# A two-block transformer layer pair on one core: the first projection begun chunk by chunk in all eight PSUM banks

## The chip, the core and the metric

One core of one Trainium2 chip runs the whole kernel. The metric is the device time of one execution in microseconds (us). The engines are TensorE (PE; its weight loads are listed as PEld), VectorE (DVE), ScalarE (ACT), GpSimd (POOL) and SyncE (SP, which here only issues DMAs).

## The reference, cut to what matters

Two layers run one after the other on 256 tokens of width 2048, all float32. The change lies in the front of the first layer:

```python
mod = silu(c) @ w_ada + b_ada                      # c: 2048, w_ada: 2048 x 6144
shift, scale, gate = split(mod, 3)
h = rms_norm(x, g_norm) * (1 + scale) + shift      # x: 256 x 2048
proj = h @ w_in                                    # w_in: 2048 x 9296
qa, ka, va, za, q_idx, k_idx, w_idx, qb, kb, vb, zb = split(proj)
# ka, qa, kb, qb, k_idx are rms-normalised per head; q_idx, k_idx, w_idx score the keys, the
# 64 best stay; two attentions, gates silu(za), silu(zb), @ w_out, residual
```

The second layer (mixer with forgetting attention, pooling, a convolutional feed-forward block) is not touched.

## The kernel before, in words

**Number format.** A float32 product is made of three faster ones. `wload` (L193) loads a weight tile of 128 x 1024 by one DMA on SP's queue into one of 8 raw buffers `wr` (L186), ACT copies it into a rounded high part `wh` (L198), and DVE subtracts for a low part `wl` (L199); there are 4 buffers of each. Activations are split in the same way into pairs `ap`. `mm3` (L222) then issues three matmuls: high x high (L226), high x low (L227), low x high (L228).

**The modulation.** `ada(col)` (L345) computes 128 columns of `mod`: two loads of 512 KB of `w_ada` (`wr`, L348), and for each a multiply-and-sum on DVE (L349, tile `junk`) against `cB`, the vector silu(c) spread over the partitions by PE (L321) and DVE (L322). `make_h(k)` (L358) builds chunk k (128 of the 2048 features) of h: two small sums (L353), the normed x times the gain (`xh`, L362), high part and full value on ACT (L364, L365), low part on DVE (L366). Chunk k needs the columns k and 16 + k, so four loads, 2.1 MB.

**The norm.** x arrives in four loads (L465). ACT squares 16 chunks (L248), PE sums them by products with a matrix of ones (L269), ACT and DVE make 1/sqrt (L273 to L280).

**The first projection.** The 16 chunks are cut into groups of 3, 4, 4 and 5 (`KS`, L37). Within a group the output is made block by block, 512 columns each: two blocks of q_idx (`fq_block`, L417), then ten of ka, qa, va, kb, qb (`tm_block`, L396), each over all chunks of the group. PSUM has eight banks: four `mm` (L177), two `sc` (L180), two `tp` (L183). The sums of ka stay in `sc` and `tp` through all groups; every other block takes two of the `mm` banks and is added to a copy in SBUF at the end of each group (`acc_add`, L373: a copy on ACT, L376, in the first group, an addition on DVE, L379, afterwards). `merge` (L439) spreads the `ada` and `make_h` steps of the next group evenly between the blocks of this one, so that a group starts with all its chunks of h.

**After it.** In the last group `ki_block` (L429, k_idx and w_idx) comes first, then q_idx and the ten blocks, with the index scores (L504), the eight rounds that find the 64 best keys (`topk_round`, L528) and the head norms (L539) between the blocks; then the gates za in eight pieces (`z_chunk`, L609), vb, attention, and the rest.

The order on each engine is chosen at build time by a scheduler that simulates the program; `keep` (L160) pins an instruction to its place in the source. Each engine executes its instructions in that order, and a wait holds up all behind it.

Of the kernel before, what the change touches and what calls it, by code (L numbers as in the profile page):

```python
# [11 lines left out]
F32 = mybir.dt.float32  # L12
# [135 lines left out]
def tile_hybrid_layers(ctx: ExitStack, tc: tile.TileContext, i: dict, out: bass.AP, dbg=None):  # L148
# [12 lines left out]


# [30 lines left out]
    def wload(src, n=1024):  # L193

        r_ = wraw(src, n)
        h = wp.tile([P, 1024], F32R, name="wh", tag="wh", bufs=HI)
        lo = wp.tile([P, 1024], F32R, name="wl", tag="wl", bufs=LO)
        nc.scalar.copy(h[:, :n], r_[:, :n])  # L198
        nc.vector.tensor_tensor(lo[:, :n], r_[:, :n], h[:, :n].bitcast(F32), op=ALU.subtract)  # L199
        return h, lo  # L200

# [109 lines left out]
    for _ in range(8):  # L311
        nc.tensor.matmul(ps[:, :P], ones, ones, start=True, stop=True)
# [4 lines left out]
    for j in range(4):  # L317
        ps = ps_mm()
        for q in range(4):
            k = 4 * j + q  # L320
            nc.tensor.matmul(ps[:, q * P:q * P + P], sc[:, 1, k:k + 1].to_broadcast([P, P]), ident, start=True, stop=True)  # L321
        nc.vector.tensor_scalar(cB[:, j // 2, (j % 2) * 512:(j % 2) * 512 + 512], ps, 0.5, None, op0=ALU.mult)  # L322
# [16 lines left out]
    nc.vector.tensor_scalar(qg[:, 0:1], v("qna"), P ** -0.5, None, op0=ALU.mult)  # L339
    nc.vector.tensor_scalar(qg[:, 1:2], v("qnb"), P ** -0.5, None, op0=ALU.mult)  # L340
# [4 lines left out]
    def ada(col):  # L345

        for hf in range(2):
            w = wraw(i["wada"][col, hf])  # L348
            nc.vector.tensor_tensor_reduce(junk[hf], w, cB[:, hf, :], 1.0, 0.0, op0=ALU.mult, op1=ALU.add,  # L349
                                           accum_out=mpart[:, col, hf:hf + 1])  # L350
# [7 lines left out]
    def make_h(k):  # L358
        mod_sum(k, 1)
        mod_sum(16 + k, 1)  # L360
        x = tmp("xh")[:, :T]
        nc.vector.scalar_tensor_tensor(x, r[:, k, NM:], v("gnorm", k), RINV[0], op0=ALU.mult, op1=ALU.mult)  # L362
# [4 lines left out]
        hA[k] = (h, lo)  # L367

# [12 lines left out]
    early = {}  # L381

    def k_tiles(src, k0, n):

        k = k0
        while k < k0 + n:
            m = min(2, k0 + n - k)
            yield [(k + j, j * 512) for j in range(m)], early.pop((id(src), k), None) or w_at(src, k, m)
            k += m
# [26 lines left out]

    def fq_block(g, b, src, k0, n):  # L417
# [21 lines left out]
    def merge(a, b):  # L439

        done = 0
        for n, f in enumerate(a):
            want = (n + 1) * len(b) // len(a)
            while done < want:
                b[done]()
                done += 1
            f()

    def group_steps(g):
        k0, n = KGROUPS[g]  # L450
        st = [lambda b=b: fq_block(g, b, w1q[b], k0, n) for b in range(2)]
        tm = [lambda b=b: tm_block(g, TMB[b // 2][0], b % 2, i["w1t"][b], k0, n) for b in range(10)]
        return st + tm

    def ada_steps(g):
        def last(k):
            ada(16 + k)
            make_h(k)

        k0, n = KGROUPS[g]  # L460
        return [f for k in range(k0, k0 + n) for f in (lambda k=k: ada(k), lambda k=k: last(k))]

    w1q = [i["w1q"][b] for b in range(2)]
    for j in range(4):
        nc.sync.dma_start(r[:, 4 * j:4 * j + 4, NM:], i["xT"][:, 4 * j:4 * j + 4, :])  # L465
    warm_ln()
    RINV[0] = rsqrt_of((square(r[:, k, NM:], T) for k in range(KC)), KC, T)
    st = ada_steps(0)
    for f in st[:-1]:
        f()  # L470
    early[id(w1q[0]), 0] = w_at(w1q[0], 0, 2)
    st[-1]()
# [6 lines left out]
    steps = group_steps(NG - 1)  # L479
# [57 lines left out]
    heads = {}  # L537

    def head_norm(key, gain):  # L539

        nss = sp.tile([P, 16], F32, name="nss", bufs=2)
        nrs = sp.tile([P, 16], F32, name="nrs", bufs=2)
        for blk in range(2):
            for f in range(2):
                a = acc[key, blk, f].rearrange("p a b -> p (a b)")
                for h in range(4):
                    sqt = tmp("sq")
                    at = blk * 8 + f * 4 + h
                    nc.scalar.activation(sqt[:, :P], a[:, h * P:h * P + P], AF.Square, accum_out=nss[:, at:at + 1])
        nc.vector.tensor_scalar(nss, nss, 1.0 / P, EPS, op0=ALU.mult, op1=ALU.add)  # L550
        nc.gpsimd.tensor_tensor(nrs, nss, neghalf, op=ALU.pow)
        for blk in range(2):
            av = [acc[key, blk, f].rearrange("p a b -> p (a b)").rearrange("p (h d) -> p h d", h=4) for f in range(2)]
            for f in range(2):
                at = blk * 8 + f * 4
                nc.vector.tensor_tensor(av[f], av[f], nrs[:, at:at + 4, None].to_broadcast([P, 4, P]), op=ALU.mult)
            for pr in range(2):
                t = ps_t()
                for h in range(2):
                    for f in range(2):  # L560
                        nc.tensor.transpose(t[:, h * T + f * 128:h * T + f * 128 + 128], av[f][:, 2 * pr + h, :], ident)  # L561
                d = bank("hT")
                nc.scalar.activation(d.rearrange("p a b -> p (a b)"), t, AF.Copy, scale=gain)
                heads[key, 4 * blk + 2 * pr] = d[:, 0, :]
                heads[key, 4 * blk + 2 * pr + 1] = d[:, 1, :]

# [6 lines left out]
    for s_ in steps[:4]:  # L573
        s_()
    ki_transpose()
    blocks = steps[4:]
    ih = 0
    for b in range(8):
# [9 lines left out]
        if 4 <= b < 8:  # L588
            topk_round()
            topk_round()  # L590
        if b == 0:
            head_norm("ka", v("kna"))
        if b == 2:
            head_norm("qa", qg[:, 0:1])
        if b == 6:
            head_norm("kb", v("knb"))
    topk_end()
# [53 lines left out]
    for zi in range(8):  # L651
        z_chunk(zi)
    for b in range(2):
# [55 lines left out]
    nc.vector.tensor_scalar(bqs, v("bq", 0, 8), P ** -0.5, None, op0=ALU.mult)  # L709
# [158 lines left out]
    nc.vector.tensor_scalar(hb, v("bga", 0, 32), 0.5, None, op0=ALU.mult)  # L868
# [210 lines left out]
```

## Time and profile before

| | |
|---|---|
| median of 3 runs | 1965.72 us (1965.16 to 1966.75) |
| the profiled execution, its own time | 1966.43 us |
| its span in the trace | 1964.7 us |
| PE busy | 1930.4 us (98%) |
| DVE busy | 1316.2 us (67%) |
| ACT busy | 975.7 us (50%) |
| mean granted TensorE clock | 0.992 of full speed |
| chain that ended last | PE 96%, DVE 2%, DMA 1% |

The execution's own time is 1.7 us above its span, and 0.7 us above the median of the runs. Matmuls are pipelined: the row of one gives its time in the pipe, and what it costs in a stream is the step from one start to the next. A float32 product that is not split shows as two rows. Times within the trace count from the start of the span.

### The profile page before, as it was taken

To read this page: it belongs to the slowest core of one execution; us is meant where nothing else is said; L and a number is where in the kernel's file an instruction comes from. 1 tells how busy PE (TensorE), PEld (TensorE's weight loads), DVE (VectorE), ACT (ScalarE), POOL (GpSimd) and SP (SyncE) were. 2 spreads that over 40 slices of the span, in tenths; PEclk is the share of its full clock that TensorE was granted. 3 is DMA by queue.
4 is the path that set the end of the run, shared out by engine and by line. 5 is a ranking of instruction groups with operands and counts; after the bars stand their busy time and mean duration, and the time that the engine had idled before them with its cause. 6 is when DMAs were issued, how large, how long until landed. Compare 5 with 4: busy or idle time off the path is not lost.

```text
span 1964.7 us, 34265 instructions
## 1 busy us (share of the span) xinstructions
PE 1930.4 (98%) x13760; PEld 1810.9 (92%) x13760; DVE 1316.2 (67%) x2063; ACT 975.7 (50%) x1537; POOL 19.4 (1%) x27
## 2 busy tenths in 40 slices
PE   6999999999999999999999999999999999999997
PEld 5888878889999999999999998999998899999886
DVE  7899788786675445755546648877764467777544
ACT  4644376466464445544444446644444454545542
POOL 0000011000000000000000000000000000000000
PEclk7999999999999999999999999999999999999999
DMA  9999685774555444556666664556666655555662
GB/s 340 353 348 348 215 265 180 286 279 148 173 165 161 140 146 130 176 183 183 183 182 183 182 182 140 185 181 183 182 184 192 193 185 181 181 182 183 206 190 87
DMA packets 126367, 391.35 MB, mean 199 GB/s; under 512 B 14400, under 2 KB 16576, under 8 KB 126208
## 3 DMA queue, kind: packets, MB, share of 16 engines
q1 hardware_dynamic: 125552, 387.83, 61.6%
q8 instruction: 108, 1.77, 0.4%
q10 hardware_dynamic: 576, 1.05, 0.1%
q14 instruction: 51, 0.42, 0.1%
q0 software_dynamic: 80, 0.28, 0.0%
HBM read 387.01 MB, written 2.10 MB: 198 GB/s over the span
## 4 chain that ended last, share of the span: by engine, by line
PE 96%; DVE 2%; DMA 1%; issue 0%; ACT 0%; SPq 0%; DVEq 0%
PE mm L226 29%; PE mm L227 29%; PE mm L228 29%; DMA wr<-in_wada_dram 1%; DVE junk L349 1%; PE sc L227 1%; PE sc L226 1%; PE tp L227 1%; PE tp L226 1%; PE tp L228 1%; PE sc L228 1%; PE tp L561 0%; PE sc L622 0%; PE tp L639 0%; PE sc L510 0%
## 5 line engine op out<-in xcount | busy, mean ns | idle before, releaser
L198 ACT CAST wh<-wr 128x1024 fp32r<-128x1024 f32 (+1 forms) x649 | 669.1, 1033 | 820.8 <-issue 320.6
L199 DVE TENSOR_TENSOR wl<-wr,wh 128x1024 fp32r<-128x1024 f32 (+1 forms) x649 | 777.8, 1201 | 444.3 <-ACT wh L198 442.0
L226 PE MATMUL mm<-ap,wh 128*128 128x258 f32 (+2 forms) x3552 | 1014.3, 286 | 13.7 <-ACT wh L198 10.7
L227 PE MATMUL mm<-ap,wh 128*128 128x258 f32 (+2 forms) x3552 | 1012.9, 285 | 0.3 <-DVE ap L366 0.3
L228 PE MATMUL mm<-ap,wl 128*128 128x258 f32 (+2 forms) x3552 | 1009.5, 285 | 2.9 <-DVE wl L199 2.9
L226 PEld LDWEIGHTS mm<-ap,wh 128*128 128x128 f32 x3552 | 674.3, 190 | 16.7 <-ACT wh L198 11.6
L228 PEld LDWEIGHTS mm<-ap,wl 128*128 128x128 f32 x3552 | 671.6, 189 | 4.6 <-DVE wl L199 3.9
L227 PEld LDWEIGHTS mm<-ap,wh 128*128 128x128 f32 x3552 | 667.2, 188 | 2.0 <-DVE ap L366 0.6
L227 PE MATMUL mm<-wl,ap 128*128 128x512 f32 x672 | 263.9, 393 | 0.5 <-DVE wl L199 0.5
L228 PE MATMUL mm<-wh,ap 128*128 128x512 f32 x672 | 262.7, 391 | 0.0
L226 PE MATMUL mm<-wh,ap 128*128 128x512 f32 x672 | 256.1, 393 | 0.0
L227 PEld LDWEIGHTS mm<-wl,ap 128*128 128x128 f32 x672 | 126.3, 188 | 27.8 <-issue 1.0
L226 PEld LDWEIGHTS mm<-wh,ap 128*128 128x128 f32 x672 | 126.2, 188 | 27.4 <-issue 1.0
L228 PEld LDWEIGHTS mm<-wh,ap 128*128 128x128 f32 x672 | 126.3, 188 | 27.2 <-issue 1.0
L349 DVE CUSTOM_DVE_ANT_0 junk<-wr,cB 128x1024 bf16<-128x1024 f32 x96 | 116.3, 1218 | 16.2 <-DMA wr<-in_wada_dram 16.2
L971 DVE TENSOR_TENSOR ca<-mm,rinv 128x258 f32<-128x258 f32 x84 | 35.8, 427 | 40.3 <-PE mm L228 40.3
L705 DVE TENSOR_TENSOR pj<-mm,rinv 128x258 f32<-128x258 f32 (+1 forms) x64 | 27.7, 432 | 42.7 <-PE mm L228 42.7
L973 ACT ACTIVATE co<-ca,vec 128x256 f32<-128x256 f32 x88 | 52.2, 598 | 0.0
L379 DVE TENSOR_TENSOR acc<-mm,acc 128x512 f32<-128x512 f32 x60 | 39.8, 682 | 9.6 <-PE mm L228 9.6
L975 DVE SCALAR_TENSOR_TENSOR co<-ca,vec,co 128x256 f32<-128x256 f32 x88 | 42.5, 484 | 2.7
L974 DVE SCALAR_TENSOR_TENSOR co<-ca,vec,co 128x256 f32<-128x256 f32 x88 | 41.9, 479 | 0.0
L878 DVE SCALAR_TENSOR_TENSOR gm<-gm,mm 128x258 f32<-128x258 f32 x32 | 13.6, 424 | 16.1 <-PE mm L228 16.0
(258 smaller groups left out, 1089.7 us busy)
## 6 DMA issues: line engine op xcount, KB each, us to landing
wr<-in_wup_dram SPq DMA_DIRECT2D x176, 512.0 KB, 3.7
wr<-in_w_dram SPq DMA_DIRECT2D x128, 512.0 KB, 3.6
wr<-in_wada_dram SPq DMA_DIRECT2D x96, 512.0 KB, 5.8
wr<-in_wdn_dram SPq DMA_DIRECT2D x88, 512.0 KB, 3.6
wr<-in_w1t_dram SPq DMA_DIRECT2D x70, 512.0 KB, 5.2
wr<-in_w1z_dram SPq DMA_DIRECT2D x32, 512.0 KB, 4.2
wr<-in_wout_dram SPq DMA_DIRECT2D x32, 512.0 KB, 3.7
wr<-in_wo_dram SPq DMA_DIRECT2D x32, 512.0 KB, 3.8
```

Of the source, the lines that this page charges most:

```text
L198: nc.scalar.copy(h[:, :n], r_[:, :n])
L199: nc.vector.tensor_tensor(lo[:, :n], r_[:, :n], h[:, :n].bitcast(F32), op=ALU.subtract)
L226: nc.tensor.matmul(ps, l[0], r_[0], start=start, stop=False)
L227: nc.tensor.matmul(ps, l[0], r_[1], start=False, stop=False)
L228: nc.tensor.matmul(ps, l[1], r_[0], start=False, stop=stop)
L349: nc.vector.tensor_tensor_reduce(junk[hf], w, cB[:, hf, :], 1.0, 0.0, op0=ALU.mult, op1=ALU.add, accum_out=mpart[:, col, hf:hf + 1])
L379: nc.vector.tensor_tensor(d, ps, d, op=ALU.add)
L705: nc.vector.tensor_tensor(t[:, :n], ps[:, :n], rinv[:, off:off + n], op=ALU.mult)
L971: nc.vector.tensor_tensor(a[:, :TQ], ps[:, :TQ], rinv, op=ALU.mult)
L973: nc.scalar.activation(o, a[:, 2:TQ], AF.Identity, scale=v("cw", 2 * 88 + ch), bias=v("cb", ch))
L974: nc.vector.scalar_tensor_tensor(o, a[:, 1:TQ - 1], v("cw", 88 + ch), o, op0=ALU.mult, op1=ALU.add)
L975: nc.vector.scalar_tensor_tensor(o, a[:, 0:T], v("cw", ch), o, op0=ALU.mult, op1=ALU.add)
```

## The change

Nine edits. (1) x is loaded first, then the first four `w_ada` tiles, with a part of the small vectors between them; c is loaded on ACT's queue. (2) ACT squares x in eight pieces of 512 elements; two of them are added to others on DVE, so that 12 sums are left for PE; 13 products that nobody reads follow, in a bank of their own. Five instead of eight products warm PE at the start. (3) Chunks 0, 1 and 2 of h are made in a fixed order on DVE, ACT and SP. The low parts of the first two weight tiles come after chunk 1 of h. (4) In each group ka and qa (four blocks, eight banks) are made chunk by chunk (`quad`), then q_idx and the other six blocks as before. (5) For chunks 0 and 1 the two qa blocks take float32 products of the unsplit weights (`whole`). (6) The modulation steps of the next group are placed by a time table that reaches into the next group's chunk-by-chunk part (`ahead`, `run`). (7) The two small sums of a chunk become one. (8) The last group begins with ka and qa, then the head norm of ka, then `ki_block`. (9) Four of the eight rounds for the best keys move behind the first four `z_chunk`s.

```diff
+    nc.scalar.dma_start(sc[:, 0, :], i["cT"])
     nc.scalar.preload_act_table_set("exp_and_others")
-    nc.sync.dma_start(sc[:, 0, :], i["cT"])
-    nc.gpsimd.dma_start(vec, i["vec"])
+    for j in range(4):
+        nc.sync.dma_start(r[:, 4 * j:4 * j + 4, NM:], i["xT"][:, 4 * j:4 * j + 4, :])
+    nvec = VEC["cw"][0]
+    w00 = []
+    for c in (0, 16):
+        w00 += [wraw(i["wada"][c, hf]) for hf in range(2)]
+        if c == 0:
+            nc.sync.dma_start(vec[:, :nvec], i["vec"][:, :nvec])
...
-    for _ in range(8):
+    for _ in range(5):
         nc.tensor.matmul(ps[:, :P], ones, ones, start=True, stop=True)
...
+    def make_h(k, x, between=lambda k: None):
+        nc.vector.tensor_reduce(mod[:, k:k + 17:16], mpart[:, k:k + 17:16, :], axis=AX.X, op=ALU.add)
         h, lo = act_pair(T)
+        between(k)
         nc.scalar.activation(h[:, :T], x, AF.Identity, scale=mod[:, 16 + k:17 + k], bias=mod[:, k:k + 1])
...
+        def step(k):
+            if k == k0:
+                begin()
+            if (k - k0) % 2 == 0:
+                load(k)
+            for b in range(4):
+                if (b, k) in whole:
+                    for hf in range(2):
+                        ps = pss[TMB[b // 2][0], b % 2, hf]
+                        nc.tensor.matmul(ps, hX[k][:, hf * 128:hf * 128 + 128], whole[b, k], start=k == k0, stop=k == k0 + n - 1)
+                    continue
+                w, o = tiles.pop((b, k))
+                for hf in range(2):
+                    key = (TMB[b // 2][0], b % 2, hf)
+                    mm3(pss[key], cut(hA[k], slice(hf * 128, hf * 128 + 128)), cut(w, slice(o, o + 512)),
+                        k == (0 if key in resident else k0), k == (KC if key in resident else k0 + n) - 1)
+            if k == k0 + n - 1:
+                for key, ps in pss.items():
+                    if key not in resident or g == NG - 1:
+                        acc_add(key, ps, g)
...
+    with in_order(DVE, ACT, nc.sync.engine):
+        warm_ln()
+        sqs = []
+        for j in range(8):
+            q = bank("sq")
+            nc.scalar.activation(q, r[:, 2 * j:2 * j + 2, NM:], AF.Square)
+            if j >= 4 and j % 2 == 1:
+                with tc.issue_after(cb_ins.ins):
+                    nc.vector.tensor_tensor(sqs[-1], sqs[-1], q, op=ALU.add)
+            else:
+                sqs.append(q)
+        ps = ps_t()
+        nsum = [q[:, j, :] for q in sqs for j in range(2)]
+        for j, q in enumerate(nsum):
+            nc.tensor.matmul(ps[:, :T], ones, q, start=j == 0, stop=j == len(nsum) - 1)
+        idle = ps_mm()
+        for _ in range(13):
+            keep(nc.tensor.matmul(idle[:, :T], ones, nsum[0], start=True, stop=True))
...
+        nc.scalar.activation(t, ps[:, :T], AF.Ln, bias=eps, scale=1.0 / D)
+        nc.scalar.activation(y, t, AF.Exp, scale=-0.5)
+        nc.scalar.activation(t, y, AF.Square)
+        ada(0, w00)
...
+        x0 = scaled(0)
+        ada(16, w00)
+        later = []
+        hX[0] = make_h(0, x0, lambda k: later.extend(groups[0][1](k)))
+        whole_weights(0)
+        for e in ada_steps(1):
+            e()
+        for f in later:
+            f()
+        whole_weights(1)
+        for e in ada_steps(2):
+            e()
...
     for g in range(NG - 1):
-        merge(group_steps(g), ada_steps(g + 1))
+        k0, n = KGROUPS[g + 1]
+        length = 16.6 * KGROUPS[g][1]
+        a = (5.5 * KGROUPS[g][1] if g == 0 else 5.5 * (KGROUPS[g][1] - 1))
+        z = length + 5.5 * (n - 1) - 9
+        ahead += [(t + a + (z - a) * (j + e / 2) / (n - 0.5), k0 + j, f) for j in range(n) for e, f in enumerate(ada_steps(k0 + j))]
+        t += length
...
+    at = run(groups[NG - 1][0][:KS[-1]], ahead, at)
...
+    head_norm("ka", v("kna"))
+    kiw = ki_block()
...
     for zi in range(8):
         z_chunk(zi)
+        if zi < TOPK // 8 - 4:
+            topk_round()
+    topk_end()
```

New helpers that the core calls: `in_order` chains the instructions of the named engines in source order without semaphores; `between(k)` at chunk 0 is `load_first`, which loads the first two ka tiles (two chunks, 512 KB each) and casts them on ACT, and returns their DVE subtractions as `later`; `whole_weights(k)` loads two float32 tiles of 256 KB into buffers of their own; `scaled(k)` is line L362 as a step; `run` calls the steps of `ahead` before a block once their time is reached, or once the block needs their chunk. Several small DVE operations on the vectors (L339, L340, L709, L868) are pinned to their places in the source.

## Rows read from the trace of the kernel before

**Rows 1.** The page, parts 1 and 4: busy time, and shares of the chain.
```profile
PE 1930.4 (98%) x13760; PEld 1810.9 (92%) x13760; DVE 1316.2 (67%) x2063; ACT 975.7 (50%) x1537; POOL 19.4 (1%) x27
...
PE 96%; DVE 2%; DMA 1%; issue 0%; ACT 0%; SPq 0%; DVEq 0%
```
**Rows 2.** Stages: length, busy by engine, granted clock, DMA share, GB/s.
```profile
10.00:40.00 30.00, 14.26 (x58) 11.72 (x57) 27.44 (x56) 11.29 (x22) 0.00 (x0) 0.63 1.03 396
...
42.00:219.00 177.00, 176.99 (x886) 149.69 (x886) 163.08 (x252) 91.63 (x117) 0.00 (x0) 1.00 0.95 340
```
**Rows 3.** Waits of PE, first 220 us: total, times, longest.
```profile
PE mm L226 <- ACT wh L198: 10.7, 1, 10.7
PE mm L226 <- ACT ap L364: 2.8, 1, 2.8
```
**Rows 4.** Timeline of PE to 62 us: start, length, what.
```profile
8.14 7.07 PE L269 MATMUL tp<-sq,ones 128*128 128x256 f32 x32
25.96 0.58 PE L226 MATMUL mm<-ap,wh 128*128 128x256 f32 x1 [10.75 <-ACT wh L198]
...
42.16 0.28 PE L228 MATMUL mm<-ap,wl 128*128 128x256 f32 x1
...
45.46 0.28 PE L228 MATMUL mm<-ap,wl 128*128 128x256 f32 x1
45.58 0.40 PE L226 MATMUL sc<-wh,ap 128*128 128x512 f32 x1
...
49.72 0.39 PE L226 MATMUL sc<-wh,ap 128*128 128x512 f32 x1
```
**Rows 5.** Single microseconds, columns as in rows 2.
```profile
15.00:16.00 1.00, 0.21 (x1) 0.00 (x0) 1.00 (x3) 0.72 (x2) 0.00 (x0) 1.00 1.02 406
...
18.00:19.00 1.00, 0.00 (x0) 0.00 (x0) 1.00 (x3) 0.00 (x0) 0.00 (x0) 0.53 1.06 422
...
42.00:43.00 1.00, 1.00 (x11) 1.00 (x11) 0.00 (x0) 0.57 (x2) 0.00 (x0) 1.00 1.04 403
```
**Rows 6.** Timeline of DVE to 42 us.
```profile
12.12 1.23 DVE L349 CUSTOM_DVE_ANT_0 junk<-wr,cB 128x1024 bf16<-128x1024 f32 x1 [2.87 <-DMA wr<-in_wada_dram]
...
23.58 1.22 DVE L349 CUSTOM_DVE_ANT_0 junk<-wr,cB 128x1024 bf16<-128x1024 f32 x1
...
24.73 1.22 DVE L349 CUSTOM_DVE_ANT_0 junk<-wr,cB 128x1024 bf16<-128x1024 f32 x1
...
35.53 1.23 DVE L199 TENSOR_TENSOR wl<-wr,wh 128x1024 fp32r<-128x1024 f32 x1 [0.27 <-ACT wh L198]
36.67 0.42 DVE L366 TENSOR_TENSOR ap<-xh,ap 128x256 fp32r<-128x256 f32 x1
...
38.15 0.69 DVE L199 TENSOR_TENSOR wl<-wr,wh 128x512 fp32r<-128x512 f32 x1
38.76 0.48 DVE L362 SCALAR_TENSOR_TENSOR xh<-r,vec,rinv 128x256 f32<-128x256 f32 x1
```
**Rows 7.** Issues on SP's queue, first of them.
```profile
0.81 0.39 SPq L295 DMA_DIRECT2D sc<-in_cT_dram  x1
1.25 2.35 SPq L465 DMA_DIRECT2D r<-in_xT_dram  x4
```
**Rows 8.** The page, part 6: a load of 512 KB in a quieter stage.
```profile
wr<-in_wup_dram SPq DMA_DIRECT2D x176, 512.0 KB, 3.7
```
**Rows 9.** Groups of instructions by line and shape: ACT to 45 us.
```profile
L198 ACT CAST wh<-wr 128x1024 fp32r<-128x1024 f32 x3 | 3.1, 1041 | 1.5 <-DMA wr<-in_w1q_dram 1.1 <-PE mm L227 0.4
...
L364 ACT ACTIVATE ap<-xh,mod 128x256 fp32r<-128x256 f32 x3 | 1.8, 600 | 12.1 <-DVE xh L362 6.3 <-DVE mod L353 5.7
```
**Rows 10.** The same view, all engines to 480 us: addition out of PSUM.
```profile
L379 DVE TENSOR_TENSOR acc<-mm,acc 128x512 f32<-128x512 f32 x60 | 39.8, 682 | 9.6 <-PE mm L228 9.6
```
**Rows 11.** Waits of PE from 220 to 480 us.
```profile
PE mm L436 <- ACT ki L433: 1.3, 1, 1.3
PE mm L228 <- DVE wl L199: 1.2, 1, 1.2
```

More of the change, by code (lines that the diff above doesn't have):

```diff
@@ L200, in wload, with wload_parts @@
         return h, lo
+    def wload_parts(src, n=1024):
+        r_ = wraw(src, n)
+        h = wp.tile([P, 1024], F32R, name="wh", tag="wh", bufs=HI)
+        lo = wp.tile([P, 1024], F32R, name="wl", tag="wl", bufs=LO)
+        nc.scalar.copy(h[:, :n], r_[:, :n])
+        return (h, lo), lambda: nc.vector.tensor_tensor(lo[:, :n], r_[:, :n], h[:, :n].bitcast(F32), op=ALU.subtract)
     def act_pair(n, first=None):
@@ L471, in tile_hybrid_layers, with ada_steps, last @@
-    early[id(w1q[0]), 0] = w_at(w1q[0], 0, 2)
-    st[-1]()
-    for g in range(NG - 1):
-        merge(group_steps(g), ada_steps(g + 1))
+        st, load = quad(g, k0, n)
+        st += [(1.38 * n, k0 + n - 1, lambda b=b: fq_block(g, b, w1q[b], k0, n)) for b in range(2)]
+        st += [(1.38 * n, k0 + n - 1, lambda b=b: tm_block(g, TMB[b // 2][0], b % 2, i["w1t"][b], k0, n)) for b in range(4, 10)]
+        return st, load
+    def ada_steps(k):
+        def last():
+            x = scaled(k)
+            ada(16 + k)
+            hX[k] = make_h(k, x)
+        return [lambda: ada(k), last]
@@ new lines, in run @@
+    def run(steps, ahead, at):
+        for cost, k, f in steps:
+            while ahead and (ahead[0][0] < at + cost or ahead[0][1] <= k):
+                ahead.pop(0)[2]()
+            f()
+            at += cost
+        return at
+    w1q = [i["w1q"][b] for b in range(2)]
+    DVE, ACT, PE = nc.vector.engine, nc.scalar.engine, nc.tensor.engine
+    groups = [group_steps(g) for g in range(NG)]
+    with in_order(DVE, ACT, nc.sync.engine):
[7 more added lines that the diff above has]
+                    nc.vector.tensor_tensor(sqs[-1], sqs[-1], q, op=ALU.add)
+            else:
+                sqs.append(q)
[6 more added lines that the diff above has]
+            keep(nc.tensor.matmul(idle[:, :T], ones, nsum[0], start=True, stop=True))
+        y, v_, t = (tmp(n)[:, :T] for n in ("rinv", "rv", "rt"))
+        nc.scalar.activation(t, ps[:, :T], AF.Ln, bias=eps, scale=1.0 / D)
+        nc.scalar.activation(y, t, AF.Exp, scale=-0.5)
+        nc.scalar.activation(t, y, AF.Square)
+        ada(0, w00)
+        nc.vector.tensor_scalar(v_, ps[:, :T], 1.0 / D, EPS, op0=ALU.mult, op1=ALU.add)
+        nc.vector.scalar_tensor_tensor(t, t, -0.5, v_, op0=ALU.mult, op1=ALU.mult)
+        RINV[0] = pair("rinv1", (P, T))
+        nc.vector.scalar_tensor_tensor(RINV[0], t, 1.5, y, op0=ALU.add, op1=ALU.mult)
+        x0 = scaled(0)
+        ada(16, w00)
+        later = []
+        hX[0] = make_h(0, x0, lambda k: later.extend(groups[0][1](k)))
[3 more added lines that the diff above has]
+        for f in later:
+            f()
+        whole_weights(1)
+        for e in ada_steps(2):
+            e()
+        nc.sync.dma_start(vec[:, nvec:], i["vec"][:, nvec:])
@@ L475, in tile_hybrid_layers @@
+    ahead = []
+    t = 0
+    for g in range(NG - 1):
+        k0, n = KGROUPS[g + 1]
[4 more added lines that the diff above has]
+        t += length
+    at = 0
+    for g in range(NG - 1):
+        at = run(groups[g][0], ahead, at)
         if g == 0:
@@ L480, in tile_hybrid_layers @@
+    at = run(groups[NG - 1][0][:KS[-1]], ahead, at)
+    steps = [f for _, _, f in groups[NG - 1][0][KS[-1]:]]
+    keep(nc.vector.tensor_scalar(qg[:, 0:1], v("qna"), P ** -0.5, None, op0=ALU.mult))
+    keep(nc.vector.tensor_scalar(qg[:, 1:2], v("qnb"), P ** -0.5, None, op0=ALU.mult))
+    head_norm("ka", v("kna"))
     kiw = ki_block()
@@ L571, in next_gate @@
             ada(gate_cols.pop(0))
-    for s_ in steps[:4]:
+    for s_ in steps[:2]:
         s_()
     ki_transpose()
-    blocks = steps[4:]
+    blocks = steps[2:]
     ih = 0
-    for b in range(8):
+    for b in range(6):
         blocks[b]()
```

164 lines of the change are left out of this document (91 added, 73 removed).

## The prediction, made before the change was timed

> **What bounds the kernel now.** I read the page first: PE is busy 98% of the span and makes 96% of the chain that ended last [rows 1], so only PE's lost time can be won back. Then the stages: from 42 to 219 us PE is busy 176.99 of 177 us at the full clock, while from 10 to 40 us it is busy 14.26 of 30 us at 0.63 of it [rows 2]. Then PE's waits: nearly all that it loses in the first 220 us is 10.7 us until the first cast weight tile and 2.8 us until a later chunk of h [rows 3]. The timeline shows the edges: the sums of squares run from 8.14 to 15.2, the first real product starts at 25.96 [rows 4]. PE is idle from 15.2; the granted clock is full in the next microsecond and about half from 18 to 19, which is the lower level, 1.2 GHz [rows 5]. It is full again after 42.
>
> Since PE is full afterwards, I reduce the opening to one number: when it would have had to start, at full clock and without a wait, to be where it is at 45.58, when both q_idx blocks of the first group are done. They are 2 x 4 x 3 x 3 = 72 products of 256 columns; 28 steps take 42.16 to 45.46, so .118 us each, 8.5 us in all. **Equivalent start before: 37.1 us.** A product of 512 columns costs .23 (18 steps from 45.58 to 49.72) [rows 4].
>
> DMA and DVE are near their limits too: from 10 to 40 us the DMA engines are fully busy at 396 GB/s, I take .40 MB/us; from 42 to 219 DVE is busy 163.08 of 177 us, 92%, the DMA engines 0.95 [rows 2].
>
> **Part by part.** *Loads (edit 1).* I count in units of 512 KB, 1.31 us each. Before, the first w_ada half, 5.55 units in with x and the vectors, was there at 12.12 [rows 6]: landing = 4.85 + 1.31 x units. x is now issued at .81 in place of 1.25 [rows 7], so 4.4 + 1.31 x units. In the new order: x 4, w_ada 4, vectors .2, two ka tiles 2 (10.2 units, landed 17.8), two whole tiles 1, chunk 1's w_ada 4 (15.2 units, 24.3), whole tiles 1, chunk 2's 4.
>
> *Norm (edit 2).* Sixteen products with ones took 7.07 us, .44 each [rows 4]; four and three warm-up products fewer put the end of the sums near 12.5. The root follows in some 2.5 us of ACT and DVE. The 13 unread products cost 13 x .44 = 5.7 us, to 18.2, inside a time in which PE has nothing else; if h came sooner they would stand in its way, at most 1 us. The two additions on DVE lie ahead of its first w_ada tile.
>
> *Chunk 0 (edits 3 to 5).* On ACT the two casts stand ahead of h by the fixed order: 17.8 + 1.04 + .60 [rows 9] = 19.4. DVE has the modulation sums by 17.5 and is no bound. PE then has 4 high x high, 4 low x high at .23 and 4 whole products. A float32 product of 512 columns is not in the trace; bounds are .44 (the 256-column one) and 2 x .44 = .88, and I take .88, since it has twice the columns. Sum 5.4 us, to 24.8. The high x low products wait for `later`. Eight whole products cost 7.0 us against 24 x .23 = 5.5: 1.5 us more on PE, in time that it would wait anyway. With no such wait it is lost in full.
>
> *Chunk 1.* The last w_ada half lands at 24.3; DVE needs 1.15 for it (23.58 to 24.73 in rows 6), then sum and ACT: 26.1. The delayed subtractions, 1.14 each [rows 6], follow the low part of h, at 28.2 and 29.35. PE has 5.4 us and then 8 products for both chunks' low parts, 1.8: 33.3.
>
> *Chunk 2.* DVE goes on without a pause with two sums and xh: 32.1. The last two halves reuse, if buffers go round, those of the ka tiles, which are free at 28.2 and 29.35; a load needs 3.7 [rows 8], so 33.1 at the latest, and SP's queue, vectors and next weights included, stands behind that issue. DVE ends at 34.4, h is there at 35.1. PE: 24 x .23 = 5.5, to 40.6. Four subtractions of .61 [rows 6] lie beside it.
>
> By 40.6 PE has done what cost 72 x .23 = 16.5 before. **Equivalent start after: 24.1, a lead of 13.0 us.** PE idles 1.2, 1.3 and 1.8 us on the way, each shorter than the idle time after which the clock fell [rows 5], so I count the full clock.
>
> *Every later group.* The chunk part holds all four `mm` banks. The first bank's last product ends 9 x .23 = 2.1 us before the part does; its addition takes .68 [rows 10], so q_idx finds a bank unless DVE is behind by more than one operation of 1.15. I take .5 us in each of three groups, bounds 0 and 2.4: **−1.5** (0 to −7). In the first group ACT copies, with time to spare: nothing.
>
> *The time table (edits 6, 7).* DVE's work to the end of the third group is the 163 us of rows 2 and four sums of 1.15 more, 168 us, now in some 166; but the steps of the last chunks, up to 4 x 5.6 us, may run in the last group's chunk part, where the deadline is later: (168 − 22)/166 = 88%. Moving them costs nothing as long as this cover holds.
>
> *The last group (edits 8, 9).* The same products in another order. PE's waits there are 1.3 at `ki_block` and 1.2 for a low part [rows 11]. Bounds: the first goes, +1.3; both come twice, −2.5. I take the middle, **−.6**. The key rounds move under `z_chunk`s, whose results are wanted 20 us later: nothing. The pinned vector operations: nothing, DVE waits there anyway.
>
> **Sum:** 13.0 − 1.5 − .6 = 10.9 us. The profiled execution took 1966.43, .7 above the median, and would take 1955.5; against the median it is 1965.72 − 10.9 = **1954.8**.
>
> **Rivals.** *The clock falls between the chunks.* For: after 15.2 it fell within 4 us, and PE now works in three pieces with pauses; 1.8 us is my sum, not a measurement. Against: the pauses are shorter than that. If chunk 1 runs at half, its 7.2 us take 14.4, to 40.5; chunk 2 then ends near 46, a lead of 7.6, less 2.1: 1960.2. The Trainium skill ("TensorE: Matmul & The Clock Gate", section "HAM oscillation — how this bites in real kernels") says that a kernel whose work on one K-tile is shorter than the wait for the next starts every K-tile at the half rate, and advises to run through K first, as the kernel before does. By that rule 1960.2 holds; rows 5 agree with the falling, and nothing in this trace shows it for so short a pause. I give it 13 in 100.
>
> *The lead is paid back.* DVE and DMA are near full [rows 2], and the lead asks both to do the same in less time; w_ada loads stand in one queue with the weights. If 8 us or more return as waits for low parts between 42 and 250 us, the time is 1963 to 1966. Against: the deadlines of the last chunks move back. 10 in 100.
>
> *Slower: h comes late in every chunk part.* If the table does not run ahead, a chunk needs on DVE four sums, three small steps and four subtractions, 5.6 + 2.4 = 8.0 us, against PE's 5.5: 2.5 us in each of 13 chunks, 33 us, 1987. It decides from about six late chunks. Against: DVE is 8% free, and before, no such wait shows. 7 in 100.
>
> *Cheaper than I count:* no wait at the banks, and that at `ki_block` gone: 13.0 + 1.3, 1951.4. 10 in 100.
>
> **How the numbers follow.** The forecast has 60 in 100; its own range is 1951.5 to 1959. The range that holds 8 in 10 reaches to the cheap case and the clock rival: 1950 to 1962. A measurement can tell .2%, 3.9 us, from no change: faster takes the forecast, the cheap case and the clock rival, .83; same .10; slower .07.
>
> **What would show it.** Right: PE's first real product near 19.4, the clock full throughout from there, two pauses of 1 to 2 us before 36, q_idx's first product near 41, PE full to the end of the projection, which comes some 11 us earlier. Wrong: a granted clock near half between 20 and 45; waits of PE on `wl` or on h behind `junk` in the later chunk parts; waits on the addition L379 where q_idx starts; a first product well after 20, which would put the loads' order in doubt.

## The result: slower by 16 us, and the profile after

The changed kernel took 1982.21 us (median of 4 runs, 1981.0 to 1982.94) beside 1966.01 us of the kernel before on the same chip (4 runs): a ratio of 1.0081 with a 95% interval of 1.007 to 1.0093. Forecast was 1954.8, so 27.4 us are to be explained. The profiled execution took 1982.94 us, its span is 1981.2.

Two marks say where to look. The first `z_chunk` begins its tanh at 343.8 us, 1.1 us earlier than before (344.9): by then most of the lead of the opening is gone, but nothing is lost. The residual of the first layer (line L827, L680 before), 32 additions behind `w_out`, begins 19.9 us later than before (510.5 against 490.6), and its last addition starts 17.0 us later (597.9 against 580.9); the span ends 16.5 us later. So the loss lies between 344 and 510 us, in a stage that the prediction costed at nothing, and about 3 us of it come back in `w_out` (more of that in experiment 12).

The stages of the changed kernel. Columns as in [rows 2]: length, busy time of PE, its weight loads, DVE, ACT and POOL, granted clock, DMA share, GB/s. The first two lines answer to rows 2, the third is the stage of the loss:

```profile
10.00:40.00 30.00, 25.18 (x89) 16.67 (x87) 23.90 (x45) 9.58 (x16) 1.72 (x2) 0.94 0.98 367
...
42.00:219.00 177.00, 174.08 (x883) 146.96 (x882) 159.75 (x235) 88.21 (x110) 0.00 (x0) 0.99 0.95 335
360.00:440.00 80.00, 65.79 (x319) 52.30 (x319) 53.16 (x108) 30.73 (x59) 0.00 (x0) 0.91 0.68 223
```

The same 80 us of the kernel before:

```profile
360.00:440.00 80.00, 78.36 (x479) 69.34 (x478) 66.65 (x133) 41.38 (x79) 0.00 (x0) 1.00 0.85 305
```

PE was idle for 14.2 of 80 us there, and the clock fell to a mean of 0.91; before it was idle for 1.6. No engine is near its limit, and the DMA engines are less busy than before (0.68 against 0.85). That is the picture of a chain of waits.

PE's waits of the changed kernel, in total, times and longest, first to 220 us (against [rows 3]) and then from 210 to 480 us (against [rows 11]):

```profile
PE mm L501 <- ACT xh L398: 3.1, 1, 3.1
PE mm L249 <- DVE wl L213: 2.0, 2, 1.4
PE sc L249 <- DVE wl L213: 1.6, 1, 1.6
...
PE mm L248 <- ACT wh L212: 7.5, 4, 2.8
PE tp L783 <- DVE p L780: 3.5, 3, 1.6
PE mm L249 <- DVE wl L213: 3.1, 5, 1.1
PE mm L534 <- ACT ki L531: 2.7, 1, 2.7
```

PE waits for high and low parts of weights and for the attention's `p`. Behind these, from 360 to 450 us, ACT and DVE wait for loads, the next two lines; in the kernel before (350 to 440 us) the same two waits were the last two lines, and ACT waited most for PE to free a buffer:

```profile
ACT wh L212 <- DMA wr<-in_w1v_dram: 24.6, 9, 6.8
DVE junk L377 <- DMA wr<-in_wada_dram: 18.1, 8, 5.1
```

```profile
DVE junk L349 <- DMA wr<-in_wada_dram: 7.9, 4, 3.0
...
ACT wh L198 <- DMA wr<-in_w1v_dram: 0.5, 2, 0.3
```

Loads that come late while the DMA engines are a third idle are loads that were issued late: their raw buffers were not free. SP's queue shows it: from 347 to 409 us it issues two loads of `w_ada` and one of vb's weights (start, length, what, count), then, in the worst rounds, nothing for 4 to 6 us, and again:

```profile
363.39 1.46 SPq L204 DMA_DIRECT2D wr<-in_wada_dram  x2
365.67 0.38 SPq L204 DMA_DIRECT2D wr<-in_w1v_dram  x1
370.39 1.46 SPq L204 DMA_DIRECT2D wr<-in_wada_dram  x2
372.67 0.38 SPq L204 DMA_DIRECT2D wr<-in_w1v_dram  x1
...
402.81 0.38 SPq L204 DMA_DIRECT2D wr<-in_w1v_dram  x1
408.94 2.79 SPq L204 DMA_DIRECT2D wr<-in_wada_dram  x2
```

What holds the buffers is one line of the change that its description ahead of the prediction does not name:

```diff
-    def ada(col):
+    def ada(col, ws=None):
         for hf in range(2):
-            w = wraw(i["wada"][col, hf])
+            w = ws.pop(0) if ws else wraw(i["wada"][col, hf])
...
+            if hf == 0 and ws is None:
+                keep(x)
```

The sum over the first half of every column of `w_ada` keeps its place in the source behind the DVE instruction written before it; the sum over the second half is free. The 16 gate columns (32 to 47) are wanted only at `w_out`; the source has five of them between the last group's blocks and eleven between the tiles of vb, behind the attention's work. The scheduler moves the free second halves to where their tile has landed, but the pinned first halves move with the work that they are tied to. DVE's order in the program, sums alone (`junk_150` is a first half, `junk_151` a second, `wr` numbers rise with the order of the loads):

```
477 junk_151 <- wr_3755      501 junk_151 <- wr_3968
482 junk_151 <- wr_3810      505 junk_151 <- wr_3992
487 junk_151 <- wr_3834      518 junk_151 <- wr_4047
490 junk_150 <- wr_3752      530 junk_150 <- wr_3807
493 junk_151 <- wr_3889      532 junk_150 <- wr_3831
497 junk_151 <- wr_3913      540 junk_151 <- wr_4077
```

The first half in `wr_3807` was loaded ahead of `wr_3810`, whose sum is number 482; its own is number 530. In between its raw buffer is held, and so are those of the first halves loaded after it. The trace lets one count them: the 22 sums that DVE makes after 347 us are those of the 22 halves loaded after it; until 408.9 SP issues 16 of these loads, and DVE makes nine of the sums, the last at 401.55. So from 402.8 to 408.9 seven of the eight buffers hold tiles whose sums come later, and one is left for vb's weights. DVE waits meanwhile, and when it comes to the sums it waits for no load:

```profile
407.69 1.23 DVE L213 TENSOR_TENSOR wl<-wr,wh 128x1024 fp32r<-128x1024 f32 x1 [4.35 <-ACT wh L212]
...
410.16 1.22 DVE L377 CUSTOM_DVE_ANT_0 junk<-wr,cB 128x1024 bf16<-128x1024 f32 x1
```

Weights and the other halves share what is left, and each round of loads waits for the last one to be used up.

The opening went largely as forecast in its first part. PE, start, length and what (against [rows 4]; a float32 product that is not split shows as two rows):

```profile
20.10 0.51 PE L248 MATMUL sc<-wh,ap 128*128 128x512 f32 x1 [0.48 <-ACT ap L397]
...
21.14 3.60 PE L501 MATMUL mm<-wn,xh 128*128 128x512 f32 x8
27.87 5.08 PE L501 MATMUL mm<-wn,xh 128*128 128x512 f32 x8 [3.13 <-ACT xh L398]
...
40.39 0.50 PE L249 MATMUL sc<-wl,ap 128*128 128x512 f32 x1 [1.59 <-DVE wl L213]
...
46.68 0.28 PE L248 MATMUL mm<-ap,wh 128*128 128x256 f32 x1
```

The first real product starts at 20.10 (forecast 19.4), and a whole product costs 3.60 / 4 = .90 us (forecast .88). But q_idx begins at 46.68 instead of near 41. Less the 16.5 us that the same work cost before, the equivalent start is 30.2, and the lead 6.9 us rather than 13.0. Single microseconds of the changed kernel (against [rows 5]):

```profile
26.00:27.00 1.00, 0.00 (x0) 0.00 (x0) 0.51 (x3) 0.42 (x1) 0.00 (x0) 1.00 1.06 422
27.00:28.00 1.00, 0.13 (x1) 0.14 (x1) 0.15 (x1) 0.78 (x2) 0.00 (x0) 0.64 1.02 410
28.00:29.00 1.00, 1.00 (x2) 0.48 (x3) 1.00 (x2) 0.00 (x0) 0.00 (x0) 0.50 1.01 401
...
42.00:43.00 1.00, 1.00 (x4) 0.81 (x3) 0.14 (x1) 0.93 (x1) 0.00 (x0) 0.50 0.95 326
```

The clock did fall to the lower level, 1.2 GHz, behind the pause of 3.1 us ahead of chunk 1, and once more behind that of 1.6 us in chunk 2.

### The profile page after: what moved, and what is told of

Read it like the earlier page. It is cut to its first block, busy times and chain, and to the rows that moved or that the text cites. A ratio compares the mean times of both kernels' runs of the same rounds, so it can differ in the third digit from the quotient of the medians.

```text
span 1981.2 us, 34242 instructions
## 1 busy us (share of the span) xinstructions
PE 1940.4 (98%) x13764; PEld 1810.7 (91%) x13764; DVE 1315.4 (66%) x2046; ACT 973.5 (49%) x1528; POOL 22.9 (1%) x26
## 4 chain that ended last, share of the span: by engine, by line
PE 91%; DMA 3%; DVE 3%; ACT 1%; issue 1%; SPq 0%; DVEq 0%
PE mm L248 28%; PE mm L249 28%; PE mm L250 28%; DMA wr<-in_wada_dram 3%; DVE wl L213 1%; DVE junk L377 1%; DMA wr<-in_w1v_dram 1%; PE sc L249 1%; PE tp L249 1%; PE tp L250 1%; PE sc L250 1%; PE sc L248 1%; PE tp L248 1%; ACT wh L212 0%; PE tp L646 0%
```

## The experiments

Medians are of the runs named; ratios are to the kernel before on the same chip, which took 1966.0 to 1967.0 us in each lot. The span is that of the profiled execution. Each edit also lets the scheduler order the whole program anew, so that a difference in time can come from another place than the one edited; where the profile shows such a place, it is named.

### 1. The gate columns unpinned

```diff
-            if hf == 0 and ws is None:
+            if hf == 0 and ws is None and col < 32:
```

> The changed kernel, but the first half of a modulation sum is pinned to its place in the source only for the columns of the projection (below 32), not for the 16 gate columns that are summed during z_chunk, vb and attention. Theory A (the pin holds back the first half of each gate column on DVE while the second half runs ahead, the waiting halves fill up to 6 of the 8 raw weight buffers, and the vb weights come one at a time): the 20 us that are lost between the start of z_chunk and w_out vanish, time 1961 to 1965, PE idle from 360 to 440 us under 3 us. Rival B (the four key rounds moved behind z_chunk make attention late): stays at 1979 to 1983. Rival C (the earlier front only shifts waits of the same total): stays above 1975.

Measured: 1963.68 us (10 runs, 1962.63 to 1964.86), ratio 0.9988 (0.9979 to 0.9998). The stage of the loss in this kernel:

```profile
360.00:440.00 80.00, 78.22 (x464) 68.11 (x462) 66.80 (x137) 43.03 (x85) 0.00 (x0) 1.00 0.80 293
```

PE is as busy as before the change. Sixteen pins cost 18.5 us. At the start of the residual it is 22.9 us (487.6 against 510.5); the rest comes back in `w_out`, which is about 3 us shorter in the changed kernel.

The opening shows something else here. The pause in chunk 2 is the same as in the changed kernel, but the granted clock stays at 1.00 from 41 to 44 us, and q_idx begins 1.4 us earlier:

```profile
40.53 0.51 PE L249 MATMUL sc<-wl,ap 128*128 128x512 f32 x1 [1.59 <-DVE wl L213]
...
45.25 0.28 PE L248 MATMUL mm<-ap,wh 128*128 128x256 f32 x1
```

### 2. The same pins in the kernel before

```diff
-            nc.vector.tensor_tensor_reduce(junk[hf], w, cB[:, hf, :], ...)
+            x = nc.vector.tensor_tensor_reduce(junk[hf], w, cB[:, hf, :], ...)
+            if hf == 0 and col >= 32:
+                keep(x)
```

> The kernel before, with one thing of the change: the first half of each gate column's sum is pinned to its place in the source. Theory A: slower by 12 to 22 us, 1978 to 1988, with PE idle in the vb stage and ACT waiting for w1v loads. Rivals B and C: no change, 1964 to 1968.

Measured: 1974.63 us (4 runs, 1972.67 to 1978.18), ratio 1.0046 (1.0031 to 1.0061).

```profile
360.00:440.00 80.00, 69.65 (x374) 56.99 (x374) 57.25 (x108) 33.48 (x61) 0.00 (x0) 0.98 0.81 263
```

The pins alone, with nothing else of the change, take 8.7 us of PE's time from this stage and 8.5 us of the whole. The place and the sign are as expected, the size of the whole is under the 12 to 22 us expected. Up to the residual the loss is 13.4 us (504.0 against 490.6); `w_out` is again about 3 us shorter than in the kernel before. That is still less than the 22.9 us in the changed kernel: what the pins cost differs with the work that they are tied to, though no run isolates this.

### 3. The key rounds in the last group again

```diff
-            topk_round()
-            topk_round()
+            for _ in range(4):
+                topk_round()
...
+    topk_end()
     head_norm("qb", qg[:, 1:2])
...
     for zi in range(8):
         z_chunk(zi)
-        if zi < TOPK // 8 - 4:
-            topk_round()
-    topk_end()
```

> The changed kernel, with all eight key rounds back before the head norm of qb, none behind z_chunk. Theory A: 1979 to 1985, as the changed kernel. Rival B: 1962 to 1968.

Measured: 1976.13 us (2 runs, 1975.89 and 1976.36), ratio 1.0052 (1.0032 to 1.0072); PE is busy 71.19 of the 80 us. That lies between both forecasts: the rounds are not the main cause, but where edit 9 puts them costs 6.1 us here. The residual begins 7.4 us earlier than in the changed kernel (503.1), and `w_out` takes as long in both.

### 4. No pin on any sum

```diff
-            if hf == 0 and ws is None:
-                keep(x)
```

> The changed kernel without any pin on the modulation sums, those of the projection included. Theory A: the vb stage is mended as in the run with the gate columns free, so 1960 to 1966; if the pins of the projection help there, it is up to 3 us slower than that run, if they hold back low parts, up to 3 us faster. Rivals B and C: above 1975.

Measured: 1960.03 us (10 runs, 1958.11 to 1963.99), ratio 0.9973 (0.9963 to 0.9982), 3.7 us less than experiment 1. In the opening, q_idx begins earlier:

```profile
39.24 0.50 PE L249 MATMUL sc<-wl,ap 128*128 128x512 f32 x1 [0.45 <-DVE wl L213]
...
43.95 0.28 PE L248 MATMUL mm<-ap,wh 128*128 128x256 f32 x1
```

With the pins two sums for the next group stood ahead of chunk 2's subtractions on DVE as far as 39.65; without, the subtractions start at 38.50, and the pause of 1.6 us shrinks to .45. Of the 2.7 us to the changed kernel 1.3 came with these pins; the other 1.4 are the second fall of the clock, which is missing in experiment 1 as well. The lead is kept afterwards: the first tanh of `z_chunk` begins at 335.9 us, 9.0 us ahead of the kernel before; in experiment 1 it begins at 341.1, in the changed kernel at 343.8. So most of what the changed kernel loses between the opening and `z_chunk` goes with the pins on columns 0 to 31: with them, in experiment 1, the lead falls from 8.35 us at q_idx to 3.8 at the tanh, without them from 9.65 to 9.0. The lead of the opening is 37.1 − (43.95 − 16.5) = 9.65 us. The next experiments begin from this kernel where nothing else is said.

### 5. Nine raw buffers, with the pins

```diff
-RAW, HI, LO, PAIRS = 8, 4, 4, 44
+RAW, HI, LO, PAIRS = 9, 4, 4, 44
```

> The changed kernel with its pins, and nine raw weight buffers in place of eight. Theory A (waiting first halves hold the raw buffers, two or three are left for the weights): one buffer more lets one load more be in flight, so a third of the 18 us that the gate pins cost goes: 1972 to 1979. Rival (the pinned sums harm by their place in DVE's order, in front of what attention needs): 1980 to 1984.

Measured, on the changed kernel: 1978.47 us (3 runs, 1976.58 to 1979.73), ratio 1.0064 (1.0047 to 1.008); PE is busy 68.05 of the 80 us. One buffer more gives 3.7 us back, a fifth of what the gate pins cost and not the third that was expected; the three runs lie below the four of the changed kernel, though the intervals of the two ratios overlap. That held buffers are what the loads wait for is borne out; that nothing of the cost comes from the place of the sums in DVE's order is not shown by this run.

### 6. PE at work through the pause ahead of chunk 1

```diff
+                        if k == 0 and b == 3 and hf == 1:
+                            for _ in range(7):
+                                keep(nc.tensor.matmul(ps[:, :T], ones, RINV[0], start=True, stop=True))
```

Seven unread products are added; the real ones start their bank anew.

> The changed kernel without pins, with seven products of ones put into the last qa bank before its first real product, so that PE works through its pause between chunks 0 and 1. If the half clock after that pause costs what its 3 us suggest, 1.5 us: 1957.5 to 1959.5, granted clock full from 20 to 48 us. If chunk 2 waits for DVE and the loads in any case: 1959.5 to 1961, though the clock is full.

Measured: 1960.79 us (9 runs, 1959.54 to 1962.53), ratio 0.9976 (0.9966 to 0.9986), no gain over experiment 4. The three microseconds behind the pause, first in experiment 4, then here, and q_idx's first product here:

```profile
27.00:30.00 3.00, 2.14 (x3) 1.10 (x4) 2.16 (x3) 0.78 (x2) 0.00 (x0) 0.56 1.02 404
```

```profile
27.00:30.00 3.00, 2.64 (x7) 0.94 (x6) 1.91 (x3) 1.02 (x2) 0.00 (x0) 1.00 1.02 404
...
44.19 0.28 PE L248 MATMUL mm<-ap,wh 128*128 128x256 f32 x1
```

The clock stays full, and q_idx starts no sooner: PE is done with chunk 1 earlier and then waits 1.4 us for chunk 2's first cast tile. The half clock behind chunk 1's pause was real, and its cost was hidden.

### 7. The head norm of ka behind ki_block

```diff
-    head_norm("ka", v("kna"))
     kiw = ki_block()
...
             nc.vector.tensor_scalar(kq[:, hf, j, :], kiw[hf][:, :ID], krs[:, hf:hf + 1], None, op0=ALU.mult)
+    head_norm("ka", v("kna"))
```

> The changed kernel without pins, with the head norm of ka behind the small work of ki_block in the source. If the squares of the norm on ACT are what ki_block's copy waits for, PE's wait there falls from 1.4 to under 1 us: 1958.5 to 1960. If not: 1959.5 to 1961.

Measured: 1963.42 us (10 runs, 1962.59 to 1965.02), ratio 0.9988 (0.9978 to 0.9997): 3.4 us slower, a miss for both sides. PE's wait for `ki` is 1.3 us, and was short already in experiment 4 (1.4): the 2.7 us in the changed kernel came with the pins on columns 0 to 31 (experiment 1, which keeps them, has 2.7 too), not with the order of edit 8. No wait of PE in the profile answers to the 3.4 us; this stays open.

### 8. Without the thirteen unread products

```diff
-        idle = ps_mm()
-        for _ in range(13):
-            keep(nc.tensor.matmul(idle[:, :T], ones, nsum[0], start=True, stop=True))
```

> The changed kernel without pins and without the 13 unread products. If they pay by the clock: PE idle from 13.9 to 20.3, half clock for the first products of chunks 0 and 1, and the end of the chunk part of the first group 1 to 5 us later: 1961 to 1965. If chunk 0's products wait for loads anyway and the lost clock is hidden: 1959 to 1961.

Measured: 1959.82 us (6 runs, 1958.18 to 1960.61), ratio 0.9967 (0.9955 to 0.9979): the same as experiment 4. The clock falls earlier and is back earlier:

```profile
14.00:20.00 6.00, 0.29 (x1) 0.29 (x2) 4.21 (x9) 3.97 (x7) 0.02 (x1) 0.69 1.04 394
20.00:24.00 4.00, 4.00 (x8) 2.25 (x8) 3.67 (x7) 0.29 (x1) 0.00 (x0) 0.61 1.03 407
24.00:32.00 8.00, 6.71 (x19) 3.20 (x18) 6.67 (x11) 1.20 (x2) 0.00 (x0) 1.00 1.03 407
```

Chunk 0 runs at half for the most part and still ends 1.3 us before chunk 1 is ready; chunk 1 runs at full. The products buy nothing here.

### 9. Experiments 1 and 3 together

The edits of both, with the pins on columns 0 to 31 left in.

> The changed kernel with the pin left off the gate columns, as in the run that gave 1963.7, and all eight rounds for the best keys in the last group again. With the pins these four rounds cost 6 us where edit 9 puts them (1982.2 against 1976.1). Theory (the rounds cost only because the pinned first halves stand in line behind them on DVE): without the gate pins their place is worth nothing, 1962.5 to 1965, no PE wait on the high parts of over 1 us from 360 to 440 us. Rival (edit 9 costs by itself, DVE having too much under the z_chunks): 1957 to 1960.

Measured: 1958.34 us (5 runs, 1957.81 to 1963.27), ratio 0.9962 (0.995 to 0.9975). The time is in the rival's range: with the rounds in the last group the kernel is 5.3 us faster even without the gate pins (1963.7 against 1958.3). But this is not the same loss as with them. In the two profiled executions, 3.4 us apart, the residual begins only .6 us earlier (487.0 against 487.6), and its last addition 3.6 us earlier (574.3 against 577.9): 3.0 us lie in `w_out`, far behind the rounds. Experiment 12 shows how.

### 10. The low parts of h one operation later on DVE

```diff
-    def ada(col, ws=None):
+    def ada(col, ws=None, mid=lambda: None):
...
+            if hf == 0:
+                mid()
...
-        nc.vector.tensor_tensor(lo[:, :T], x, h[:, :T].bitcast(F32), op=ALU.subtract)
+        low(lambda: nc.vector.tensor_tensor(lo[:, :T], x, h[:, :T].bitcast(F32), op=ALU.subtract))
...
-        hX[0] = make_h(0, x0, lambda k: later.extend(groups[0][1](k)))
+        low = []
+        hX[0] = make_h(0, x0, lambda k: later.extend(groups[0][1](k)), low.append)
         whole_weights(0)
-        for e in ada_steps(1):
-            e()
-        for f in later:
-            f()
+        ada(1, mid=low[0])
+        x1 = scaled(1)
+        ada(17)
+        hX[1] = make_h(1, x1, low=low.append)
+        later[0]()
+        low[1]()
+        later[1]()
```

> The changed kernel without pins, and in the fixed order on DVE the low parts of h of chunks 0 and 1 stand one operation later, behind a modulation sum or a subtraction that is ready, so that DVE does not wait 1.3 us for each. Theory (DVE's order is what keeps the opening's lead at 9.65 us): chunk 1 starts near 26.6 instead of 27.9, h of chunk 2 near 33.3 instead of 35.7, q_idx's first product near 42 to 42.7 instead of 43.95, time 1957.5 to 1959. Rival (the loads bound the opening: the last w_ada halves land no earlier): chunk 1 at 27.5 or later, q_idx within 0.4 us of 43.95, time 1959.5 to 1960.5.

Measured: 1957.53 us (5 runs, 1956.27 to 1958.36), ratio 0.9952 (0.9939 to 0.9966). The time is in the theory's range, the marks are not: q_idx begins at 43.35, .6 us earlier than in experiment 4, and the two profiled executions differ by .6 us as well (1957.53 and 1958.11). DVE (start, length, what) shows why:

```profile
21.31 1.23 DVE L377 CUSTOM_DVE_ANT_0 junk<-wr,cB 128x1024 bf16<-128x1024 f32 x1 [2.42 <-DMA wr<-in_wada_dram]
22.46 0.42 DVE L399 TENSOR_TENSOR ap<-xh,ap 128x256 fp32r<-128x256 f32 x1
...
34.78 0.16 DVE L394 TENSOR_REDUCE mod<-mpart 128x2 f32<-128x6 f32 x1
```

DVE, ready earlier, waits 2.42 us for chunk 1's first tile of `w_ada`: for chunk 1 the loads bind, and only for chunk 2 the order on DVE (the sum at 34.78 instead of 35.55). The rest of the 2.5 us between the medians is that executions of experiment 4 spread over 5.9 us and those of this one over 2.1; why is open.

### 11. Experiment 10 with a filled pause

Four unread products at the place of experiment 6.

> The run before this, with four unread products of 256 columns in PE's pause ahead of chunk 1, so that the granted clock stays full. The half clock at chunk 1 stretches its whole products by 1.5 us; when this was filled without the other order on DVE nothing came of it, which I put down to chunk 2 being late anyway. Theory (both bind together): q_idx's first product 1 to 1.5 us ahead of the run before, near 41, time 1956 to 1958. Rival (chunk 2's tiles, cast only behind h, bind): the same as the run before within 0.4 us.

Measured: 1958.52 us (5 runs, 1957.57 to 1959.13), ratio 0.9957 (0.9945 to 0.997). q_idx begins at 43.08. The clock is full and nothing is gained, for the second time; ahead of chunk 2 PE waits .39 us for a cast.

### 12. Experiment 10 with the key rounds in the last group

The edits of experiments 10 and 3.

> The changed kernel without pins, with the low parts of h one operation later on DVE (the run that gave 1957.5), and with all eight rounds for the best keys in the last group. If edit 9 costs DVE time under the z_chunks by itself, as it did with the gate pins (6.1 us) and without them (5.3 us): 1951.5 to 1954. If the place of the rounds matters only where first halves are pinned somewhere: 1956.5 to 1959.5.

Measured: 1953.14 us (5 runs, 1951.05 to 1955.24), ratio 0.993 (0.9916 to 0.9943), 4.4 us less than experiment 10. This beats both kernels; in its profile PE is busy 79.40 of the 80 us from 360 on. What the rounds' place changes first is when the mask of the best keys, `distm`, is there. DVE in the kernel before, in the changed kernel, in experiment 10, and in this one (start of the last step, and for the last two the summary of a line: durations in ns, then first and last start):

```profile
338.91 0.55 DVE L535 TENSOR_TENSOR distm<-distm,dist 128x384 f32<-128x384 f32 x1
```

```profile
395.01 0.56 DVE L712 TENSOR_TENSOR distm<-distm,dist 128x384 f32<-128x384 f32 x1
```

```profile
L716 DVE TENSOR_TENSOR distm<-distm,dist x1: 558/558/558, 382.2 to 382.2; 128x384 f32<-128x384 f32 x1
...
L791 PE MATMUL tp<-pt,acc x32: 270/273/377, 395.0 to 492.1; 128*128 128x128 f32 x32
```

```profile
L716 DVE TENSOR_TENSOR distm<-distm,dist x1: 557/557/557, 337.7 to 337.7; 128x384 f32<-128x384 f32 x1
...
L792 PE MATMUL tp<-pt,acc x32: 270/273/275, 376.6 to 490.3; 128*128 128x128 f32 x32
```

The mask is ready 44.5 us earlier than in experiment 10, and the first products of `p` with the values run at 376.6 instead of 395.0. In the two late cases the rounds themselves are over at 350 and 336 us; only the two steps of `topk_end` come so late, behind the sums for the gate columns and the low parts on DVE.

That the later attentions cost the 4.4 us is not borne out. The residual (first and last addition), and 40 us within `w_out`, in experiment 10 and then here:

```profile
L831 DVE SCALAR_TENSOR_TENSOR r<-mm,mod,r x32: 475/483/488, 481.9 to 572.2; 128x256 f32<-128x256 f32 x32
...
520.00:560.00 40.00, 40.00 (x342) 40.00 (x341) 30.80 (x48) 22.95 (x36) 0.00 (x0) 1.00 0.58 176
```

```profile
L829 DVE SCALAR_TENSOR_TENSOR r<-mm,mod,r x32: 474/482/487, 480.2 to 567.6; 128x256 f32<-128x256 f32 x32
...
520.00:560.00 40.00, 40.00 (x355) 40.00 (x355) 32.98 (x54) 24.01 (x40) 0.00 (x0) 1.00 0.59 182
```

Up to `w_out` the gain is 1.7 us; in `w_out` it is 2.9 more. There PE is busy throughout and at the full clock in both, and does 342 products of 256 columns in 40 us in one and 355 in the other: a step of .118 us against .113. No wait can show that. The profiles fall into two groups: from the first to the last addition it takes some 90.3 us in the kernel before and in experiments 1, 4, 6, 7, 8, 10 and 11, and some 87.4 in the changed kernel and in experiments 2, 3, 5, 9 and 12. Each kernel was profiled once. What sets the step stays open, whether the program or the execution, and no run shows that it has to do with the rounds.

## Why the prediction was wrong

**The pinned vector operations: "nothing, DVE waits there anyway".** This step failed, and it carries most of the error. It weighed the small pinned operations on the vectors and passed over the pin in `ada`, which, for the gate columns alone, ties 16 sums of 512 KB tiles to instructions far away. It also asked only whether DVE is short of time. DVE was not: it is busy for 53 of the 80 us from 360 on. What ran short was the raw buffers, since a tile that waits for its sum keeps its buffer: seven of the eight were held at 408 us. The gate columns' pins cost 18.5 us (experiment 1; 8.5 us when put into the kernel before, experiment 2), those of columns 0 to 31 another 3.7 us (experiment 4). A ninth buffer gave back 3.7 us. Taken off in this order, the two terms are 22.2 of the 27.4 us.

**The key rounds: "under `z_chunk`s, whose results are wanted 20 us later: nothing".** Wrong by 6.1 us with the pins (experiment 3). The mask came 56 us later than before, far more than the 20 us that the term allowed, since the last two steps stand in DVE's queue behind sums that wait for `w_ada`. Without the gate pins the same move is worth 5.3 and 4.4 us of time (experiments 9 and 12), but only .6 and 1.7 us of what the profiled executions gain lie ahead of `w_out`; the other 3 us are PE's shorter step there, whose cause is open.

**The opening, a lead of 13.0 us.** 6.9 us as the change stands, 9.65 us without the pins, 10.5 us in experiment 12 (37.1 − (43.08 − 16.5)). Its single terms against experiment 4, which has no pins: the first product .9 us later than forecast; chunk 1's products start at 27.86 instead of 26.1, since they need the full value of h, ACT's second operation, where I counted one, and since the first of its four tiles of `w_ada` has landed only at about 21.3 (experiment 10), .9 us later than my 512 KB units gave (20.4), and DVE's four sums follow from there. The whole products stretched from 3.60 to 5.13 us by the half clock. The low x high products of chunk 0, .9 us, ran behind chunk 1 rather than in chunk 0. The price of a whole product (.90 for .88) and the start of h in chunk 2 (35.74, where 35.1 was forecast for h to be there) were close, and the pauses came where they were expected. But the one ahead of chunk 1 was longer than forecast (2.9 us for 1.3), and the clock, counted as full, fell there.

**Every later group and the last one, −1.5 and −.6.** Too dear, if anything: in experiment 12 the lead is 10.5 us at q_idx and 10.4 us where the residual begins (490.6 − 480.2). No wait on the addition where q_idx starts is among PE's longer waits. At the span's end the lead is 13.3 us (1964.7 − 1951.4), but the last 2.9 are `w_out`'s shorter step, which is no term of the prediction: that experiment 12 comes within 1.7 us of the forecast time is in part luck.

**The time table: "costs nothing as long as this cover holds".** Right: no wait of PE for h in a later chunk part shows above .5 us.

**The rivals.** The clock fell between chunks, as the rival had it and as the Trainium skill says of work pieces shorter than the wait for the next ("TensorE: Matmul & The Clock Gate", section "HAM oscillation — how this bites in real kernels"). The trace agrees on the fall, though not on that condition: chunk 0's work, 20.1 to 24.7 us, is longer than the pause of 3.1 us behind it. The fall ahead of chunk 1 cost nothing where I had put 5.4 us: with the clock kept full q_idx started no earlier (experiments 6 and 11), since chunk 2 was late for other reasons. The second fall, in chunk 2 of the changed kernel, cost 1.4 us (experiment 1). Of the second rival, the lead paid back by DMA and DVE, the changed kernel shows a part: 5.8 of 6.9 us are gone at 344 us. But most of that goes with the pins, not with engines at their limits: without pins 9.0 of 9.65 us are left (experiment 4). The slower rival, h late in every chunk part, did not happen; the kernel was slower by another mechanism, in a stage that no rival touched. The forecast sign was wrong for that one reason: without the gate pins the ratio is 0.9988 (0.9979 to 0.9998), without any 0.9973.

## What to carry to other kernels

An order tie on an instruction that empties a shared buffer is a tie on everything that needs such a buffer; ask not whether its engine has time, but how many buffers stand full while it waits, and what loads next. When two halves of one job are tied differently, look at the program's order of both before costing the tie at nothing. A filler that holds the clock is worth only what comes next on the path: first see which operand the next piece waits for. And when a difference in time answers to no wait, count the instructions of a stage in both profiles before giving it a cause.

## What the runs showed of the hardware that was not expected

The clock can fall behind a short pause: in the changed kernel PE was idle from 38.8 to 40.39 us, 1.6 us, and the granted clock was .50 from 41 to 44 us. The same pause of 1.59 us in experiment 1 left it at 1.00, so the length of this pause alone does not decide. And half clock in chunk 0 instead of chunk 1 (experiment 8) gave the same time, since PE used its slack either way.

A PE that is busy throughout at a granted clock of 1.00 is not always equally fast: the step of the same 256-column products in `w_out` was .118 us in eight of the profiled executions and .113 in six, 2.9 us over the stage. No wait and no clock row shows it; the count of products in a window does.
